# Segment mean: the general path rewritten with one-hot matmuls, the verdict for its branch read before the store, and part of the table work moved to GpSimd

## The chip, the cores and the metric

One core of one Trainium2 chip. The metric is the device time of one execution in microseconds, as the median of several. A profile gives a second clock, the span of the profiled execution, from its first record to its last; the device time is 1.77 us longer than that span in the kernel before. All times "at 190.66" below are microseconds from the start of the span. Repeats of one kernel scatter by up to 1.7%, and the chips differ by about 1%, so kernels are compared by ratios to runs of the kernel before on the same chip. An execution over 1.5% above the fastest of its kernel counts as slow and is left out of the ratio.

## The reference

```python
def reference(data, segment_ids):            # 10,000,000 float32, sorted ids in [0, 10000)
    num_segments = int(segment_ids.max()) + 1
    sums = np.zeros(num_segments, dtype=np.float32)
    counts = np.zeros(num_segments, dtype=np.float32)
    np.add.at(sums, segment_ids, data)
    np.add.at(counts, segment_ids, 1)
    return sums / np.maximum(counts, 1)
```

## The kernel before

The data are laid out as 128 partitions of 78,125 values, and each partition is cut into 98 "rows" of 800 values (the last has 525). The ids are sorted, and a segment holds about 1000 values, so a row usually contains one boundary between segments. The fast path finds that boundary with little reading of the ids: it reads a few probes, GpSimd gathers one window of 159 ids per row with a software DMA (98 gathers), ScalarE sums the window (the sum tells where the boundary lies), VectorE splits the row's data there, and ScalarE sums the whole row.

```python
def gather(g):
    for r in range(bounds[g], bounds[g + 1]):
        nc.gpsimd.indirect_dma_start(out=GT[:, r % RING, :], in_=ids2d[:], ...)   # 98 of these
def add_ids(r):                               # ScalarE: sum of the gathered window
    nc.scalar.activation(out=junk_a[:, 0:W], in_=gt32[:, r % RING, 0 : 2 * W : 2], func=ACT.Relu,
                         accum_out=GS[:, r : r + 1])
def second_look(a, b):                        # VectorE: where in the row the boundary lies
    def s1():
        nc.vector.tensor_sub(out=KK[:, a:b], in0=QQ[:, a:b], in1=GS[:, a:b])
    return [s1]
def total(r): ...                             # ScalarE: sum of the row's data
def split(r):                                 # VectorE: sum of the data before the boundary
    nc.vector.scalar_tensor_tensor(out=junk_v[:, 0:n], in0=iota[:, 0:n], scalar=KK[:, r : r + 1], in1=d,
                                   op0=ALU.is_lt, op1=ALU.mult, accum_out=A[:, r : r + 1])
```

Then the sums become segment means (`counts`, `sums`), and the means find their place in the output by compares and products (`select`, `table`, `place`; the last rows by `pick`). All of it is VectorE's. `check` and `verdict` find out whether the assumptions held; if not, the general path must do everything again. The answer of `verdict` is called the verdict here. `put(r, steps, k)` interleaves these steps behind row r, k steps to a row.

```python
    # ... cut ...
    put(75, sums(48, 72) + table(8, 13) + place(0, 40), 2)
    put(82, counts(72, R1))
    put(last_look + 1, keys(72, NX)[1:] + [check])          # check: GpSimd
    put(last_look + 3, select(13, NT1 // 4))
    put(89, sums(72, R1) + table(13, NT1 // 4) + place(40, C1) + place(C1, NO), 2)
    put(91, counts(R1, R3), 3)
    put(93, pick(sel1, R1, R2, C1), 3)
    put(94, pick(sel2, R2, R3, C2) + sums(R1, R2, False), 3)
    put(95, add_rows1(), 2)
    put(96, verdict())                                       # writes badi after the last split

def finish():
    # ... cut: the last sums and the last reduce ...
    for i, (src, dst) in enumerate(own_outputs(OUT, out2d[0:1, :])):
        (nc.scalar if i % 2 else nc.sync).dma_start(out=dst, in_=src)       # the output store
    with tc.If(nc.values_load(badi[0:1, 0:1], min_val=0, max_val=1) > 0):   # not taken here
        general_path(...)     # a running scan, then a binary search with indirect DMAs on GpSimd
```

With this input the branch is never taken, so how fast the general path would run plays no part in any time below.

Of the kernel before, what the change touches and what calls it, by code (L numbers as in the profile page):

```python
# [9 lines left out]
FP32 = mybir.dt.float32  # L10
# [7 lines left out]
P = 128  # L18
D = 78125
# [19 lines left out]
R1 = 84  # L39
R2 = 94  # L40
R3 = NR + 4
C1 = 50
C2 = 58


def general_path(tc, pool, ppool, data, segment_ids, ids2d, out2d, rdram, kdram, ident):


    nc = tc.nc
    N = data.shape[0]  # L50
    CH = 125
    data_p = data.rearrange("(p d) -> p d", p=P)
    ids_p = segment_ids.rearrange("(p d) -> p d", p=P)
    run_p = rdram.rearrange("(p d) u -> p (d u)", p=P)

    prev = pool.tile([P, 1], FP32, name="g_prev")
    rprev = pool.tile([P, 1], FP32, name="g_rprev")
    first = pool.tile([P, 1], FP32, name="g_first")
    f64 = pool.tile([P, 1], I64, name="g_f64")
    nc.sync.dma_start(out=f64, in_=ids_p[:, 0:1])  # L60
    nc.vector.tensor_copy(out=first, in_=f64.bitcast(I32)[:, 0:1])
    nc.vector.memset(prev, -1.0)
    nc.vector.memset(rprev, 0.0)
    with tc.For_i(0, D, CH) as c:
        i64 = pool.tile([P, CH], I64, name="g_i64")
        idf = pool.tile([P, CH + 1], FP32, name="g_idf")
        dat = pool.tile([P, CH], FP32, name="g_dat")
        msk = pool.tile([P, CH], FP32, name="g_msk")
        run = pool.tile([P, CH], FP32, name="g_run")
        nc.sync.dma_start(out=i64, in_=ids_p[:, bass.ds(c, CH)])  # L70
        nc.sync.dma_start(out=dat, in_=data_p[:, bass.ds(c, CH)])
        nc.vector.tensor_copy(out=idf[:, 0:1], in_=prev)
        nc.vector.tensor_copy(out=idf[:, 1 : CH + 1], in_=i64.bitcast(I32)[:, 0 : 2 * CH : 2])
        nc.vector.tensor_tensor(out=msk, in0=idf[:, 1 : CH + 1], in1=idf[:, 0:CH], op=ALU.is_equal)
        nc.vector.tensor_tensor_scan(
            out=run, data0=msk, data1=dat, initial=rprev[:, 0:1], op0=ALU.mult, op1=ALU.add
        )
        nc.vector.tensor_copy(out=prev, in_=idf[:, CH : CH + 1])
        nc.vector.tensor_copy(out=rprev, in_=run[:, CH - 1 : CH])
        nc.sync.dma_start(out=run_p[:, bass.ds(c, CH)], in_=run)  # L80


    pt = ppool.tile([1, 3 * P], FP32, name="g_pt")
    nc.tensor.transpose(out=pt[:, 0:P], in_=first, identity=ident)
    nc.tensor.transpose(out=pt[:, P : 2 * P], in_=prev, identity=ident)
    nc.tensor.transpose(out=pt[:, 2 * P : 3 * P], in_=rprev, identity=ident)
    row = pool.tile([1, 3 * P], FP32, name="g_row")
    nc.vector.tensor_copy(out=row, in_=pt)
    same = pool.tile([1, P], FP32, name="g_same")
    cont = pool.tile([1, P], FP32, name="g_cont")  # L90
    kd = pool.tile([1, P + 1], FP32, name="g_kd")
    nc.vector.memset(kd, 0.0)
    nc.vector.memset(cont, 0.0)
    nc.vector.tensor_tensor(out=same, in0=row[:, 0:P], in1=row[:, P : 2 * P], op=ALU.is_equal)
    nc.vector.tensor_tensor(
        out=cont[:, 1:P], in0=row[:, 1:P], in1=row[:, P : 2 * P - 1], op=ALU.is_equal
    )
    nc.vector.tensor_mul(out=cont, in0=cont, in1=same)
    nc.vector.tensor_tensor_scan(
        out=kd[:, 1 : P + 1], data0=cont, data1=row[:, 2 * P : 3 * P], initial=0.0,  # L100
        op0=ALU.mult, op1=ALU.add,
    )
    nc.sync.dma_start(out=kdram.rearrange("(u n) v -> u (n v)", u=1), in_=kd)

    Q = 125
    pedge = pool.tile([P, P], FP32, name="g_pedge")
    pe_i = pool.tile([P, P], I32, name="g_pei")
    nc.gpsimd.iota(pe_i, pattern=[[1, P]], base=1, channel_multiplier=0)
    nc.vector.tensor_scalar(out=pedge, in0=pe_i, scalar1=float(D), scalar2=None, op0=ALU.mult)
    seg = pool.tile([P, 2], FP32, name="g_seg")  # L110
    seg_i = pool.tile([P, 2], I32, name="g_segi")
    nc.gpsimd.iota(seg_i, pattern=[[1, 2]], base=0, channel_multiplier=80)
    nc.vector.tensor_copy(out=seg, in_=seg_i)
    means = pool.tile([P, 80], FP32, name="g_means")
    pos = pool.tile([P, 2], FP32, name="g_pos")
    step = pool.tile([P, 1], FP32, name="g_step")
    with tc.For_i(0, 80, 1) as q:
        nc.vector.memset(pos, 0.0)
        nc.vector.memset(step, float(1 << 23))
        with tc.For_i(0, 24, 1):  # L120
            cand = pool.tile([P, 2], FP32, name="g_cand")
            at = pool.tile([P, 2], FP32, name="g_at")
            at_i = pool.tile([P, 2], I32, name="g_ati")
            got = pool.tile([P, 2], I64, name="g_got")
            lt = pool.tile([P, 2], FP32, name="g_lt")
            ok = pool.tile([P, 2], FP32, name="g_ok")
            nc.vector.tensor_scalar(out=cand, in0=pos, scalar1=step[:, 0:1], scalar2=None, op0=ALU.add)
            nc.vector.tensor_scalar(
                out=at, in0=cand, scalar1=-1.0, scalar2=float(N - 1), op0=ALU.add, op1=ALU.min
            )  # L130
            nc.vector.tensor_copy(out=at_i, in_=at)
            for j in range(2):
                nc.gpsimd.indirect_dma_start(
                    out=got[:, j : j + 1], out_offset=None, in_=ids2d[:],
                    in_offset=bass.IndirectOffsetOnAxis(ap=at_i[:, j : j + 1], axis=0),
                )
            nc.vector.tensor_tensor(out=lt, in0=got.bitcast(I32)[:, 0:4:2], in1=seg, op=ALU.is_lt)
            nc.vector.tensor_scalar(out=ok, in0=cand, scalar1=float(N), scalar2=None, op0=ALU.is_le)
            nc.vector.tensor_mul(out=ok, in0=ok, in1=lt)
            nc.vector.scalar_tensor_tensor(  # L140
                out=pos, in0=ok, scalar=step[:, 0:1], in1=pos, op0=ALU.mult, op1=ALU.add
            )
            nc.vector.tensor_scalar(out=step, in0=step, scalar1=0.5, scalar2=None, op0=ALU.mult)
        last = pool.tile([P, 1], FP32, name="g_last")
        idx = pool.tile([P, 2], I32, name="g_idx")
        idxf = pool.tile([P, 2], FP32, name="g_idxf")
        val = pool.tile([P, 2], FP32, name="g_val")
        cnt = pool.tile([P, 1], FP32, name="g_cnt")
        some = pool.tile([P, 1], FP32, name="g_some")
        over = pool.tile([P, 1], FP32, name="g_over")  # L150
        jnk = pool.tile([P, P], FP32, name="g_jnk")
        nc.vector.tensor_scalar(
            out=idxf[:, 0:1], in0=pos[:, 1:2], scalar1=-1.0, scalar2=0.0, op0=ALU.add, op1=ALU.max
        )
        nc.vector.tensor_scalar(
            out=jnk, in0=pedge, scalar1=idxf[:, 0:1], scalar2=None, op0=ALU.is_le, op1=ALU.add,
            accum_out=idxf[:, 1:2],
        )
        nc.vector.tensor_copy(out=idx, in_=idxf)
        nc.gpsimd.indirect_dma_start(  # L160
            out=val[:, 0:1], out_offset=None, in_=rdram[:],
            in_offset=bass.IndirectOffsetOnAxis(ap=idx[:, 0:1], axis=0),
        )
        nc.gpsimd.indirect_dma_start(
            out=val[:, 1:2], out_offset=None, in_=kdram[:],
            in_offset=bass.IndirectOffsetOnAxis(ap=idx[:, 1:2], axis=0),
        )
        nc.vector.tensor_sub(out=cnt, in0=pos[:, 1:2], in1=pos[:, 0:1])
        nc.vector.tensor_scalar(out=some, in0=cnt, scalar1=0.0, scalar2=None, op0=ALU.is_gt)
        nc.vector.tensor_scalar(out=cnt, in0=cnt, scalar1=1.0, scalar2=None, op0=ALU.max)  # L170
        nc.vector.reciprocal(out=cnt, in_=cnt)
        nc.vector.tensor_mul(out=cnt, in0=cnt, in1=some)
        nc.vector.tensor_scalar(out=last, in0=idxf[:, 1:2], scalar1=float(D), scalar2=None, op0=ALU.mult)
        nc.vector.tensor_tensor(out=over, in0=pos[:, 0:1], in1=last, op=ALU.is_lt)
        nc.vector.tensor_mul(out=over, in0=over, in1=val[:, 1:2])
        nc.vector.tensor_add(out=over, in0=over, in1=val[:, 0:1])
        nc.vector.tensor_mul(out=means[:, bass.ds(q, 1)], in0=over, in1=cnt)
        nc.vector.tensor_scalar(out=seg, in0=seg, scalar1=1.0, scalar2=None, op0=ALU.add)
# [17 lines left out]
def kernel(  # L196
# [543 lines left out]
    def finish():  # L740
        n, m = NO - C2, R3 - R2
        for f in sums(R2, R3, False):
            f()
# [118 lines left out]
```

## Time and profile before

| | |
|---|---|
| median of 3 runs | 203.19 us (201.97 to 203.42) |
| profiled execution | 204.25 us, span 202.48 us |
| VectorE (DVE) busy | 140.4 us, 69% |
| ScalarE (ACT) busy | 138.2 us, 68% |
| GpSimd (POOL) busy | 106.9 us, 53% |

No engine is busy over 70%, because the limits follow one another. From the page of the kernel before: the busy times; then busy tenths in 40 slices of about 5 us; then the costliest groups (line, engine, operation, out<-in, shape, count, busy us, mean ns, idle us before them and what ended most of it).

```profile
PE 1.6 (1%) x6; PEld 1.4 (1%) x6; DVE 140.4 (69%) x537; ACT 138.2 (68%) x393; POOL 106.9 (53%) x135
...
DVE  6526197556684856695696849758597999899700
ACT  0042698986999967596797849689695988993000
POOL 5577747772765637174745535674645758810000
DMA  6999999999999999999999999999999999900000
...
L373 POOL DMA_INDIRECT GT<-in_segment_ids_dram,IDX x98 | 98.0, 1000 | 67.6 <-ACT junk_a L383 28.6
L403 DVE SCALAR_TENSOR_TENSOR junk_v<-iota,q_120,data_t 128x800 bf16<-128x800 f32 x98 | 102.0, 1041 | 31.8 <-DMA data_t<-in_data_dram 27.4
```

For about 35 slices the DMA row is full and the splits wait for their data. Then VectorE alone runs full, and the last two slices are empty on every engine. The table of stretches of the kernel before shows the same with the borders set at three events: VectorE's last wait for data (153.9), the landing of the last data (177.9), and the issue of the output store (191.43). Its columns are the stretch, its length, busy us of each engine, the clock, the DMA share and GB/s.

```profile
core 0: us, PE busy (x) PEld busy (x) DVE busy (x) ACT busy (x) POOL busy (x), PEclk, DMA share, GB/s
0.00:153.90 153.90, 0.99 (x4) 0.93 (x4) 104.28 (x420) 110.61 (x319) 90.62 (x103) 1.00 1.06 285
153.90:177.90 24.00, 0.00 (x0) 0.00 (x0) 23.20 (x77) 21.77 (x61) 16.21 (x32) 1.00 0.99 392
177.90:191.43 13.53, 0.59 (x2) 0.50 (x2) 12.91 (x42) 5.80 (x14) 0.09 (x1) 1.00 0.00 1
191.43:202.48 11.05, 0.00 (x0) 0.00 (x0) 0.00 (x0) 0.00 (x0) 0.00 (x0) 1.00 0.03 7
```

VectorE is busy 36.1 of the 37.5 us between 153.9 and 191.43. After that, 11 us in which no engine computes. The chain of work that ended last is of no help there: it follows compute and ends with VectorE's last reduce (191.05 + 0.35 us), so the tail has to be read from the instructions of the engines' sequencers (POOLq, SPq), the parts that issue the instructions, wait on semaphores (counters by which engines wait for each other) and branch. DRAIN is the name of such an instruction in the trace. These are the ones of the branch's line in the kernel before (count, duration in ns as minimum/median/maximum, first and last start), and then the DRAINs of the program's last line.

```profile
L750 POOLq COMPARE_BRANCH  x1: 45/45/45, 190.7 to 190.7; - x1
...
L750 POOLq INC_SWDGE_SEM  x1: 2146/2146/2146, 191.4 to 191.4; - x1
...
L750 SPq TENSOR_LOAD <-badi x1: 836/836/836, 193.0 to 193.0; - x1
...
L750 SPq COMPARE_BRANCH  x1: 50/50/50, 194.2 to 194.2; - x1
```

```profile
L857 POOLq DRAIN  x3: 40/107/8081, 193.6 to 202.2; - x3
L857 SPq DRAIN  x3: 7/7/13, 195.9 to 201.9; - x3
```

GpSimd branches at 190.66, spends 2.15 us in INC_SWDGE_SEM (which, by its name, increments a semaphore of the software DMA), and then spends 8.08 us in a DRAIN, from 193.56 to 201.64. SyncE, which has to issue the store (1.06 + 0.37 us), load the verdict and check it, is ready at 196.0 and waits 5.6 us for GpSimd. Barriers of 0.84 us follow. One label misleads here: the list of waits of the DMA queue's engine puts this wait down to PE, because PE's semaphore is the last of several to come; PE had long been done (its last matmul started at 189.51).

```profile
SPq L857 <- PEq L857: 6.4, 2, 5.8
```

### The profile page before, as it was taken

How to read it: one execution, taken by the hardware profiler on the slowest of the kernel's cores; microseconds unless marked ns; L12 is line 12 of the kernel's file. 1: busy time of each engine (PE TensorE's matmuls, PEld its weight loads, DVE VectorE, ACT ScalarE, POOL GpSimd, SP SyncE). 2: the span in 40 equal slices, each digit the busy share in tenths (PEclk: the TensorE clock that was granted, in tenths of full speed). 3: DMA queues.
4: the chain of work that ended last, by engine and by line, in shares of the span. 5: the costliest groups of instructions: out<-in, count | busy, mean ns of one | idle time of the engine just before them, and what ended most of it. 6: DMA issues, size and time to landing. Idle time of an engine off the chain costs nothing.

```text
span 202.5 us, 1634 instructions
## 1 busy us (share of the span) xinstructions
PE 1.6 (1%) x6; PEld 1.4 (1%) x6; DVE 140.4 (69%) x537; ACT 138.2 (68%) x393; POOL 106.9 (53%) x135
## 2 busy tenths in 40 slices
PE   0000000000001000000000000000000000000100
PEld 0000000000001000000000000000000000000000
DVE  6526197556684856695696849758597999899700
ACT  0042698986999967596797849689695988993000
POOL 5577747772765637174745535674645758810000
DMA  6999999999999999999999999999999999900000
GB/s 98 105 117 359 255 404 241 316 338 341 250 257 406 255 326 201 400 241 282 306 314 336 209 378 238 350 310 337 307 242 390 403 407 405 395 17 2 2 12 0
DMA packets 75143, 53.41 MB, mean 264 GB/s; under 512 B 65601, under 2 KB 65684, under 8 KB 75127
## 3 DMA queue, kind: packets, MB, share of 16 engines
q1 hardware_dynamic: 70249, 40.54, 71.8%
q0 software_dynamic: 4704, 12.74, 20.7%
q14 instruction: 16, 0.13, 0.2%
q10 hardware_dynamic: 174, 0.00, 0.1%
HBM read 56.46 MB, written 0.04 MB: 279 GB/s over the span
## 4 chain that ended last, share of the span: by engine, by line
DMA 36%; SPq 29%; issue 11%; DVE 8%; ACT 7%; POOL 2%; ACTq 0%; POOLq 0%; DVEq 0%
DMA data_t<-in_data_dram 24%; SPq L247 23%; DMA GT<-in_segment_ids_dram,IDX 12%; SPq L239 6%; ACT junk_a L398 4%; DVE junk_v L403 4%; ACT junk_a L383 3%; POOL GT L373 2%; DVE shf L688 0%; DVE tab L678 0%; DVE sel L673 0%; DVE add_150 L695 0%; DVE CS L602 0%; DVE FF L608 0%; DVE add_150 L726 0%
## 5 line engine op out<-in xcount | busy, mean ns | idle before, releaser
L373 POOL DMA_INDIRECT GT<-in_segment_ids_dram,IDX x98 | 98.0, 1000 | 67.6 <-ACT junk_a L383 28.6
L403 DVE SCALAR_TENSOR_TENSOR junk_v<-iota,q_120,data_t 128x800 bf16<-128x800 f32 x98 | 102.0, 1041 | 31.8 <-DMA data_t<-in_data_dram 27.4
L398 ACT ACTIVATE junk_a<-data_t 128x800 bf16<-128x800 f32 x98 | 85.0, 867 | 17.4 <-DMA data_t<-in_data_dram 10.7
L383 ACT ACTIVATE junk_a<-GT 128x159 bf16<-128x159 int32 x98 | 33.9, 346 | 18.6 <-DMA GT<-in_segment_ids_dram,IDX 10.7
L383 ACT ACTIVATION_READ_ACCUMULATOR junk_a<-GT 128x1 f32 x98 | 18.3, 187 | 0.0
L398 ACT ACTIVATION_READ_ACCUMULATOR junk_a<-data_t 128x1 f32 x98 | 18.2, 186 | 0.0
L390 DVE TENSOR_TENSOR q_120<-QQ,GS 128x5 f32<-128x5 f32 (+1 forms) x20 | 3.2, 162 | 13.8 <-issue 9.2
L403 DVE DVE_READ_ACCUMULATOR junk_v<-iota,q_120,data_t 128x1 f32 x98 | 8.3, 84 | 0.0
L383 ACT ACT_TABLE_LOAD x1 | 1.3, 1283 | 9.7 <-DVE q_120 L335 9.7
L329 DVE TENSOR_TENSOR eq<-pr 128x20 f32<-128x20 int32 (+1 forms) x20 | 3.5, 176 | 2.5 <-DMA pr<-in_segment_ids_dram 2.4
L342 DVE TENSOR_SCALAR NB<-q_120 128x5 f32<-128x5 f32 (+1 forms) x20 | 4.3, 215 | 0.0
L338 DVE TENSOR_SCALAR ST<-jc 128x5 f32<-128x5 f32 (+1 forms) x20 | 4.1, 204 | 0.0
L331 DVE CAST q_120<-pr 128x6 f32<-128x6 int32 (+2 forms) x20 | 3.9, 196 | 0.0
L334 DVE TENSOR_REDUCE jc<-eq 128x5 f32<-128x20 f32 (+1 forms) x20 | 3.4, 172 | 0.0
L352 DVE TENSOR_TENSOR pos<-ST,wb 128x5 f32<-128x5 f32 (+1 forms) x20 | 3.4, 168 | 0.0
L335 DVE TENSOR_TENSOR q_120<-q_120 128x5 f32<-128x5 f32 (+1 forms) x20 | 3.2, 160 | 0.0
L359 DVE SCALAR_TENSOR_TENSOR IDX<-NB,pos 128x5 int32<-128x5 f32 (+1 forms) x20 | 3.2, 160 | 0.0
L363 DVE SCALAR_TENSOR_TENSOR QQ<-NB,QQ 128x5 f32<-128x5 f32 (+1 forms) x20 | 3.2, 158 | 0.0
L353 DVE SCALAR_TENSOR_TENSOR QQ<-q_120,ST 128x5 f32<-128x5 f32 (+1 forms) x20 | 3.2, 158 | 0.0
L678 DVE TENSOR_REDUCE tab<-sel 128x32 f32<-128x384 f32 (+2 forms) x3 | 1.6, 534 | 0.1
L673 DVE TENSOR_TENSOR sel<-sel,RF 128x384 f32<-128x384 f32 (+2 forms) x3 | 1.6, 535 | 0.0
L664 DVE TENSOR_TENSOR sel<-KEY,jj 128x384 f32<-128x384 f32 (+2 forms) x3 | 1.6, 535 | 0.0
(113 smaller groups left out, 40.4 us busy)
## 6 DMA issues: line engine op xcount, KB each, us to landing
data_t<-in_data_dram SPq DMA_DIRECT2D x48, 800.0 KB
GT<-in_segment_ids_dram,IDX POOLq DMA_INDIRECT x98
pr<-in_segment_ids_dram SPq DMA_DIRECT2D x18, 25.0 KB
data_t<-in_data_dram SPq DMA_DIRECT2D x1, 400.0 KB
data_t<-in_data_dram SPq DMA_DIRECT2D x1, 262.5 KB
out_dram<-OUT SPq DMA_DIRECT2D x1, 36.6 KB
pr<-in_segment_ids_dram SPq DMA_DIRECT2D x1, 21.0 KB
pr<-in_segment_ids_dram SPq DMA_DIRECT2D x1, 18.0 KB
```

Of the source, the lines that this page charges most:

```text
L239: nc.sync.dma_start(out=pr_flat[:, a:b], in_=ids_p[:, a * S : (b - 1) * S + 1 : S])
L247: nc.sync.dma_start(out=d[:, 0 : c - a], in_=data_p[:, a:c])
L329: nc.vector.tensor_tensor(out=eq, in0=in0b, in1=in1b, op=ALU.is_equal)
L331: nc.vector.tensor_copy(out=V[:, a:e], in_=pr32[:, a:e, 0])
L334: nc.vector.tensor_reduce(out=jc, in_=eq, axis=AX.X, op=ALU.add)
L338: nc.vector.tensor_scalar(out=ST[:, a:b], in0=jc, scalar1=float(S), scalar2=float(1 + W), op0=ALU.mult, op1=ALU.add,)
L342: nc.vector.tensor_scalar(out=NB[:, a:b], in0=BT[:, a:b], scalar1=1.0, scalar2=None, op0=ALU.not_equal)
L352: nc.vector.tensor_add(out=pos, in0=ST[:, a:b], in1=wb[:, a:b])
L373: nc.gpsimd.indirect_dma_start(out=GT[:, r % RING, :], out_offset=None, in_=ids2d[:], in_offset=bass.IndirectOffsetOnAxis(ap=IDX[:, r : r ...
L383: nc.scalar.activation(out=junk_a[:, 0:W], in_=gt32[:, r % RING, 0 : 2 * W : 2], func=ACT.Relu, accum_out=GS[:, r : r + 1],)
L398: nc.scalar.activation(out=junk_a[:, 0:n], in_=d, func=ACT.Copy, accum_out=t)
L403: nc.vector.scalar_tensor_tensor(out=junk_v[:, 0:n], in0=iota[:, 0:n], scalar=KK[:, r : r + 1], in1=d, op0=ALU.is_lt, op1=ALU.mult, accum_ ...
```

## The change

The general path no longer uses GpSimd's DMA: it compares the upper and lower digits of each id with a ramp (one-hot vectors) and lets TensorE add up counts and sums in a 79x256 product. Without software DMA behind the branch, and with the verdict read into registers before the end, nothing should be left to do between the store and the end. Compares and products of the last table go to GpSimd, the middle table moves to rows 64 to 73, one block of rows less is handled separately at the end, and VectorE sums the gathered ids of rows 89 to 97 itself (ScalarE still sums them too). The checks go from GpSimd to VectorE, and a small store of the first outputs goes from ScalarE's queue, behind row 75, to SyncE's, later; the lines of that store and the body of the new check are cut below.

```diff
-def general_path(tc, pool, ppool, data, segment_ids, ids2d, out2d, rdram, kdram, ident):
+def general_path(tc, pool, ppool, data, segment_ids, out2d, ramp):
     # ... cut: out go the scan, the binary search and
-                nc.gpsimd.indirect_dma_start(out=got[:, j : j + 1], in_=ids2d[:], ...)
-        nc.gpsimd.indirect_dma_start(out=val[:, 0:1], in_=rdram[:], ...)
-        nc.gpsimd.indirect_dma_start(out=val[:, 1:2], in_=kdram[:], ...)
     # ... in come, per column of data:
+                nc.vector.tensor_scalar(out=oh, in0=ramp[:, 0:HI], scalar1=hi[:, at], op0=ALU.is_equal, ...)
+                nc.vector.tensor_scalar(out=ol[:, 0:LO], in0=ramp[:, 0:LO], scalar1=lo[:, at], op0=ALU.is_equal, ...)
+                nc.vector.tensor_scalar(out=ol[:, LO : 2 * LO], in0=ol[:, 0:LO], scalar1=dat[:, at], op0=ALU.mult, ...)
+                nc.tensor.matmul(out=prod, lhsT=oh, rhs=ol, start=u == 0, stop=u == U - 1)
@@
-R1 = 84
-R2 = 94
-R3 = NR + 4
+R1 = 94
+R2 = NR + 4
+ON_ACT = 89
@@ second_look
+                nc.vector.tensor_reduce(      # rows 89 to 97
+                    out=GS[:, c:e], in_=gt32[:, s : s + e - c, 0 : 2 * W : 2], axis=AX.X, op=ALU.add)
@@ select, table, place and pick take an engine; on GpSimd a compare is a subtract and an is_equal with 0
+            e.tensor_tensor(out=out, in0=in0, in1=in1, op=ALU.subtract)
+            e.tensor_scalar(out=out, in0=out, scalar1=0.0, scalar2=None, op0=ALU.is_equal)
@@ finish
-        with tc.If(nc.values_load(badi[0:1, 0:1], min_val=0, max_val=1) > 0):
+        with tc.If(verdict_reg[0] > 0):
@@ the schedule
-    put(75, sums(48, 72) + table(8, 13) + place(0, 40), 2)
-    put(82, counts(72, R1))
-    put(last_look + 1, keys(72, NX)[1:] + [check])
-    put(last_look + 3, select(13, NT1 // 4))
-    put(89, sums(72, R1) + table(13, NT1 // 4) + place(40, C1) + place(C1, NO), 2)
-    put(91, counts(R1, R3), 3)
-    put(93, pick(sel1, R1, R2, C1), 3)
-    put(94, pick(sel2, R2, R3, C2) + sums(R1, R2, False), 3)
-    put(95, add_rows1(), 2)
-    put(96, verdict())
+    put(64, counts(48, 66), 2)
+    put(67, sums(48, 66) + table(8, 12, v) + place(0, 36, v), 2)
+    put(60, check(), 2)                                          # check: VectorE
+    put(last_look + 1, keys(MID, NX)[1:] + check_late())
+    put(last_look + 2, select(12, NT1 // 4, g))
+    put(last_look + 2, pick()[:1])
+    put(91, counts(66, R2), 3)
+    put(93, pick()[1:])
+    put(93, sums(66, R1), 4)
+    t, p = table(12, NT1 // 4, g), place(36, NO, g)
+    put(93, t[:1])
+    put(95, t[1:] + p[:1], 2)
+    put(96, p[1:])
+    put(94, verdict())
+    after[96].append(lambda: verdict_reg.append(nc.values_load(badi[0:1, 0:1], min_val=0, max_val=1)))
```

## The prediction

> **What bounds the kernel now.** Three stretches. (a) To about 154 us it runs at the pace of the loads: the splits (VectorE, 800 columns, 0.97 us start to start in the timeline) wait for data_t, 27 us in the list of waits. (b) From 153.9 to 191.4 us VectorE never waits for anything but its own previous result: the data have landed by 178 us and ScalarE ends at 183.9, but VectorE still has the tables, picks and last rows to do. (c) From the output store (191.43) to 202.5 us nothing computes. The branch's and the end's own lines show why: GpSimd starts INC_SWDGE_SEM at 191.38 (2.15 us) and then a DRAIN of 8.08 us, to 201.64; SyncE is ready at 196.0. Barriers (0.8 us) follow. So 5.6 us of the tail are GpSimd's alone.
>
> **What changes.**
> 1. No software DMA in the general path: INC_SWDGE_SEM disappears from GpSimd's program. I take the long DRAIN to belong to it (at the start of the kernel the same pair takes 0.03 and 0.17 us).
> 2. The verdict is read before the last split, so SyncE no longer does register load, checks and branch set-up (about 1.2 us) after the store. Store issue 1.49, branch and 18 semaphore waits about 1.9, barriers 0.8-1.0: tail about 4.4 us instead of 11.05. **-6.7 us.** If the DRAIN stayed 8 us it would begin some 6 us earlier with the earlier verdict, and the loss would be only about 1.5 us.
> 3. VectorE after 153.9: removed are the last select (0.57), its product (0.69), both place products (0.9), picks and adds of two blocks (about 3.5, one block of 0.75 stays), separate counts and sums of rows 72-83 and 84-93 (about 2), and the middle table, moved into the load-bound stretch (about 2.5). Added: two sums of the gathered ids on VectorE (795 and 636 elements, 0.9 and 0.75 us), check_late and two products (0.7).
> 4. But ScalarE still sums all 98 windows, so VectorE's sums of rows 89 to 97 wait for ScalarE's write. ScalarE's sum of row 93 ended at 169.8; VectorE will want it at about 167.6. VectorE should idle about 2 us there and 0.5 us before the second sum.
> 5. GpSimd gets 528-, 168- and 559-element operations. From the trace a tensor_tensor of 122 takes 0.40 and one of 1 takes 0.19 us, so about 1.75 ns an element (the Trainium skill, "GPSIMD Engine Reference", section 3.1, says about 2.6 cycles, a little slower); estimates 1.1 to 1.2 us for each large product. The place product may hold VectorE 0.3 us.
> 6. ScalarE no longer waits about 1.7 us for its small store (153.9): its end moves up by 0.5-1 us.
>
> By start-to-start times of like instructions, VectorE's last reduce ends near 188.6 instead of 191.4: **-2.8 us**.
>
> **Prediction: 194.0 us, 8 in 10 from 191.5 to 197.5.** Faster by over 2%: 0.95; within 2%: 0.04; slower: 0.01.
>
> **What would show it:** no INC_SWDGE_SEM at the end and GpSimd's last DRAIN under 1 us; end of the span 4 to 5 us after the store's issue; VectorE idle before its sums of GT; last reduce at 187.5-189.5; splits up to row 75 at unchanged times.
>
> **What would make it wrong:** the DRAIN is a cost of any software DMA (then about 195.5); GpSimd's selects run far slower than estimated and hold up the last table; the register load on VectorE stalls the last split by more than 0.2 us; ScalarE, waiting for the verdict, becomes last; the loads land later.

## The result, and the profile after

The changed kernel takes 196.28 us (195.87 to 197.04, 4 runs) against 203.31 us (201.97 to 203.77, 4 runs) of the kernel before of the same rounds. The ratio is 0.966, with a 95% interval of 0.961 to 0.971. A ratio here is the mean time of one kernel's fast runs over that of the other's of the same rounds, so not quite the ratio of these medians. In a later comparison, with six runs of it, the ratio was 0.964 (0.960 to 0.969). The prediction was 194.0 us, in a range of 191.5 to 197.5.

The lines of the page after the change that answer to those of before:

```profile
PE 1.6 (1%) x6; PEld 1.4 (1%) x6; DVE 139.9 (72%) x541; ACT 138.1 (71%) x393; POOL 108.0 (55%) x121
...
DVE  6535197874775867495967686967999679899960
ACT  0043398985999998595968686866978779999310
POOL 5487737775467573746456373737383674850410
DMA  6999999999999999999999999999999999993000
...
L290 POOL DMA_INDIRECT GT<-in_segment_ids_dram,IDX x98 | 98.3, 1003 | 66.2 <-ACT junk_a L300 31.2
L333 DVE SCALAR_TENSOR_TENSOR junk_v<-iota,q_118,data_t 128x800 bf16<-128x800 f32 x98 | 102.1, 1042 | 26.8 <-DMA data_t<-in_data_dram 23.7
```

The table of stretches of the kernel after, with the borders at the like events (the same split starts at 153.15 instead of 153.86, the store is issued at 188.97):

```profile
0.00:153.20 153.20, 0.99 (x4) 0.93 (x4) 108.12 (x444) 111.06 (x321) 90.29 (x103) 1.00 1.06 286
153.20:177.30 24.10, 0.00 (x0) 0.00 (x0) 20.98 (x64) 21.63 (x61) 14.69 (x16) 1.00 1.00 395
177.30:188.97 11.67, 0.59 (x2) 0.50 (x2) 10.75 (x34) 5.44 (x12) 3.07 (x3) 1.00 0.01 4
188.97:194.88 5.91, 0.00 (x0) 0.00 (x0) 0.00 (x0) 0.00 (x0) 0.00 (x0) 1.00 0.04 8
```

The tail has shrunk from 11.05 to 5.91 us and the two stretches before it from 37.5 to 35.8 us. The branch's line of the kernel after, and the DRAINs of its last line:

```profile
L711 POOLq COMPARE_BRANCH  x1: 45/45/45, 185.2 to 185.2; - x1
...
L711 SPq COMPARE_BRANCH  x1: 50/50/50, 190.5 to 190.5; - x1
```

```profile
L824 POOLq DRAIN  x3: 40/113/8409, 185.6 to 194.6; - x3
L824 SPq DRAIN  x3: 7/7/7, 192.0 to 194.3; - x3
```

INC_SWDGE_SEM is gone, but the long DRAIN is not: it takes 8.41 us, now from 185.62 to 194.03. (GpSimd's last product ran until 185.93, so 8.10 us of it follow GpSimd's last work, where it was 8.08 before.) SyncE is ready at 192.09, 1.94 us before GpSimd. So the end is still GpSimd's; only it starts 5.5 us earlier, and from the branch to the end it is 2.1 us shorter. In the list of waits of the DMA queue's engine, after the change:

```profile
SPq L824 <- PEq L824: 2.7, 2, 2.1
```

VectorE's last reduce ends at 188.94. What VectorE waited for from 153.3 to 188.97 in the kernel after (us in total, times, longest):

```profile
DVE junk_v L333 <- DMA data_t<-in_data_dram: 3.6, 4, 1.3
DVE GS L311 <- ACT junk_a L300: 0.5, 1, 0.5
DVE OUT L675 <- POOL shf L668: 0.4, 1, 0.4
DVE junk_v L333 <- DVE j_163 L440: 0.2, 1, 0.2
```

And in the kernel before, from 154 to 191.43 (the 1.3 us end at 153.86, at the border, so they are not inside it):

```profile
DVE junk_v L403 <- DMA data_t<-in_data_dram: 1.3, 1, 1.3
DVE q_120 L390 <- ACT junk_a L383: 0.6, 1, 0.6
```

VectorE's busy time in these two stretches fell by 4.4 us (23.20 + 12.91 against 20.98 + 10.75), but only 1.8 us of that shortened them. Work taken away before 168 us was partly turned into waits for loads: of the 3.6 us, 1.3 us lie at the border as before, and 2.3 us are new, from 155.6, 159.4 and 164.8 on. That this comes with the rearranged work is seen across the runs: all eight profiles that have it and all 98 gathers show such waits after row 76 (1.2 to 2.3 us, counting waits over 0.12 us), and the three with the old work (before, e1, e2) show none.

### The profile page after: what moved, and what is told of

Its sections match the earlier page's. It is cut to its first block, busy times and chain, and to the rows that moved or that the text cites. A ratio compares the mean times of both kernels' runs of the same rounds, so it can differ in the third digit from the quotient of the medians.

```text
span 194.9 us, 1624 instructions
## 1 busy us (share of the span) xinstructions
PE 1.6 (1%) x6; PEld 1.4 (1%) x6; DVE 139.9 (72%) x541; ACT 138.1 (71%) x393; POOL 108.0 (55%) x121
## 4 chain that ended last, share of the span: by engine, by line
DMA 31%; SPq 30%; issue 14%; DVE 10%; ACT 10%; POOL 3%; POOLq 0%; DVEq 0%; ACTq 0%
SPq L162 24%; DMA data_t<-in_data_dram 23%; DMA GT<-in_segment_ids_dram,IDX 7%; SPq L154 6%; ACT junk_a L328 5%; DVE junk_v L333 5%; ACT junk_a L300 4%; POOL GT L290 2%; POOL shf L668 1%; DVE CS L577 1%; DVE tab L658 0%; DVE GS L311 0%; DVE ct L559 0%; DVE FF L583 0%; DVE q_118 L574 0%
## 5 line engine op out<-in xcount | busy, mean ns | idle before, releaser
L695 POOL TENSOR_TENSOR pk<-pk,RB 128x168 f32<-128x168 f32 x1 | 0.5, 507 | 7.2 <-DVE q_118 L574 7.2
L259 DVE TENSOR_SCALAR NB<-q_118 128x5 f32<-128x5 f32 (+1 forms) x20 | 3.5, 176 | 0.0
L255 DVE TENSOR_SCALAR ST<-jc 128x5 f32<-128x5 f32 (+1 forms) x20 | 3.5, 174 | 0.0
L311 DVE TENSOR_REDUCE GS<-GT 128x5 f32<-128x795 int32 (+1 forms) x2 | 1.8, 899 | 0.6 <-ACT junk_a L300 0.5
L668 POOL TENSOR_TENSOR shf<-tab,dm 128x559 f32<-128x559 f32 x1 | 1.3, 1332 | 1.4 <-DVE badi L528 1.4
```

Of the source, the lines that this page charges most:

```text
L255: nc.vector.tensor_scalar(out=ST[:, a:b], in0=jc, scalar1=float(S), scalar2=float(1 + W), op0=ALU.mult, op1=ALU.add,)
L259: nc.vector.tensor_scalar(out=NB[:, a:b], in0=BT[:, a:b], scalar1=1.0, scalar2=None, op0=ALU.not_equal)
```

## The experiments

Ten runs, of nine kernels, were made on three chips, on which the kernel before took 205.74, 205.09 and 205.35 us. Ratios compare each with the kernel before on its own chip. Two events decide when each kernel ends: GpSimd's end of its long DRAIN, and SyncE's readiness. All from the profiles, in us; "work" is from the start of the split of row 76 to the end of VectorE's last reduce.

| profile | work | last reduce ends | GpSimd's DRAIN ends | SyncE ready | end of span |
|---|---|---|---|---|---|
| before | 37.54 | 191.40 | 201.64 | 196.00 | 202.48 |
| after | 35.79 | 188.94 | 194.03 | 192.09 | 194.88 |
| e1_path_only | 37.61 | 193.83 | 201.72 | 197.92 | 202.57 |
| e2_verdict_early | 38.51 | 193.35 | 193.55 | 197.17 | 198.00 |
| e3_drain_early | 35.10 | 190.69 | 187.75 | 193.84 | 194.67 |
| e4_no_dve_sums | 33.77 | 187.93 | 193.01 | 191.08 | 193.87 |
| e5_compute_only | 35.44 | 189.95 | 200.22 | 194.54 | 201.06 |
| e6_half_gathers | 35.80 | 179.41 | 180.49 | 182.55 | 183.39 |
| e7_best | 34.16 | 189.18 | 191.30 | 192.32 | 193.16 |
| e8_no_act_sums | 34.69 | 188.06 | 193.16 | 191.22 | 194.01 |
| after_again | 35.19 | 190.33 | 195.43 | 193.49 | 196.28 |
| e7_again | 34.04 | 190.12 | 192.25 | 193.27 | 194.10 |

In all twelve rows the end of the span is the later of the two events plus 0.83 to 0.86 us (after: 194.03 + 0.85; e2: 197.17 + 0.83). That is the whole account of the end of this program, and each experiment moves one or more of its terms. The main theory: the long DRAIN is owed for the 98 gathers of the fast path, whatever lies behind the branch, and it ended the kernel both before and after.

### e1_path_only: the kernel before with the new general path alone

```diff
-            general_path(tc, fpool, ppool, data, segment_ids, ids2d, out2d, rdram, kdram, ident[:, 0:P])
+            general_path(tc, fpool, ppool, data, segment_ids, out2d, iota)
```

> The kernel before with the new general path alone. Theory D: the long DRAIN of GpSimd is owed for the gathers, lasts about 8.1 us after GpSimd's last work whatever stands in the branch, and starts when GpSimd has passed the branch. Then INC_SWDGE_SEM (2.15 us) goes, the DRAIN stays at 8.0 to 8.4 us and starts near 191.2 in the span, and the time falls by 2.0 to 2.5 us (ratio to the kernel before 0.988 to 0.990). Rival I (of the prediction): the DRAIN belongs to INC_SWDGE_SEM; then the last DRAIN is under 1 us and the time falls by about 5.5 us (ratio 0.973).

Measured: 202.75 us, ratio 0.984 (0.978 to 0.990), unclear at the limit of 2%; the interval holds the 0.988 of the main theory and not the 0.973 of the prediction's reading. Its profile fell in a run that counts as slow (204.34 us, over 1.5% above the fastest), so its span is not compared, only what its end consists of. INC_SWDGE_SEM is absent behind the branch, and the DRAINs of the last line are:

```profile
L772 POOLq DRAIN  x3: 40/107/8157, 193.6 to 202.3; - x3
L772 SPq DRAIN  x3: 7/7/7, 197.9 to 202.0; - x3
```

The general path owns the 2.15 us of INC_SWDGE_SEM and not the DRAIN. From GpSimd's branch (193.10) to the end are 9.47 us, against 11.82 us in the kernel before: 2.35 us less, and 8.16 us of DRAIN are still there. The prediction's assumption that the two belong together falls.

### e2_verdict_early: the kernel before, with the verdict earlier and nothing else

```diff
-        with tc.If(nc.values_load(badi[0:1, 0:1], min_val=0, max_val=1) > 0):
+        with tc.If(verdict_reg[0] > 0):
@@
-    put(96, verdict())
+    put(91, verdict())
+    after[94].append(lambda: verdict_reg.append(nc.values_load(badi[0:1, 0:1], min_val=0, max_val=1)))
```

> The kernel before, old general path, with its verdict moved from after row 96 to after rows 91 and 92 and the register load to row 94; no work is taken from VectorE. Theory D: GpSimd passes the branch near 182 instead of 190.7, INC_SWDGE_SEM and the 8.1 us DRAIN are over near 192.5, and SyncE, ready 3.1 us after the store's issue near 191.4, becomes last: span about 195.3, time 6 to 7.5 us less than before (ratio 0.963 to 0.971), about as much as the whole change. Rival V: the change's gain comes from the work taken off VectorE and from the path; then only SyncE's register load is saved, at most 1.2 us (ratio 0.994 or more).

Measured: 199.23 us, ratio 0.968 (0.962 to 0.975), so as much as the whole change gives, with the old general path and no work taken off VectorE. GpSimd's branch moved from 190.66 to 182.55, and INC_SWDGE_SEM and the DRAIN, still 2.15 and 8.08 us long, ran beside VectorE's last rows:

```profile
L859 POOLq DRAIN  x3: 40/107/8081, 185.5 to 197.7; - x3
L859 SPq DRAIN  x3: 7/7/13, 197.1 to 197.4; - x3
```

GpSimd is done at 193.55, SyncE at 197.17. The end has changed hands. The rival, that a gain of this size needs VectorE's saved work, falls. The span of this profile, 198.00, was expected at 195.3: VectorE's last reduce came 2 us later than in the kernel before (1.0 us of it at the split of row 76 already), which was not looked into.

### e3_drain_early: the changed kernel, with a DRAIN on GpSimd in the middle

```diff
     put(last_look + 2, pick()[:1])
+    put(last_look + 2, [lambda: nc.gpsimd.drain()])
```

> The changed kernel with one more drain on GpSimd, after the compares of the last pick, where GpSimd idles from 173.6 to 180.8. Theory D: this drain takes about 8.1 us and ends near 181.7, the last one is then under 0.5 us, SyncE (192.1 in the changed kernel) is last, and the time is 1.7 to 2.3 us under the changed kernel's (ratio to the kernel before about 0.955). Rival F: a DRAIN at the end has a fixed cost; then the last one is still 8 us and the time is that of the changed kernel (0.966) or more.

Measured: 196.14 us, ratio 0.954 (0.951 to 0.957); the change itself has 0.966 and 0.964 in its two comparisons. The added DRAIN, and those of the last line:

```profile
L754 POOLq DRAIN  x1: 8780/8780/8780, 174.1 to 174.1; - x1
```

```profile
L825 POOLq DRAIN  x3: 34/112/346, 187.4 to 194.4; - x3
L825 SPq DRAIN  x3: 7/7/7, 193.8 to 194.1; - x3
```

The cost can be paid once, earlier: 8.78 us at 174.1, while GpSimd had nothing urgent to do (for 0.68 us of it the last compare still ran, so 8.10 us follow GpSimd's work, as at the end of the changed kernel), and then 0.35 us at the end (during which its last product still ended). So it is not a fixed price of ending the program. With it out of the way, the end comes 3.98 us after VectorE's last reduce (190.69 to 194.67), not the 5.94 us of the changed kernel. The prediction had 4.4 us for this tail, so its sum for SyncE's share was 0.4 us too high.

### e4_no_dve_sums: the changed kernel, with the window sums left to ScalarE alone

```diff
-ON_ACT = 89
+ON_ACT = NR
@@
-        put(a - 2 if a < ON_ACT else a - 3 if b < NR else a - 4, second_look(a, b))
+        put(a - 2 if b < NR else a - 3, second_look(a, b))
```

> The changed kernel without VectorE's sums of gathered ids for rows 89 to 97 (ScalarE's sums, which it makes anyway, are used, as in the kernel before). Theory S: those sums, their products and their waits for ScalarE cost VectorE about 2.7 us (0.90 + 0.73 + 0.43 + 0.65) on the way to the verdict and to the store; both move up by 2.0 to 2.7 us and so does the end (ratio to before 0.953 to 0.957). Rival: VectorE only waits elsewhere for ScalarE or the data; then less than 1 us is gained (0.962 or more).

Measured: 195.85 us, ratio 0.957 (0.950 to 0.964). In the changed kernel ScalarE sums the windows of rows 89 to 97 too, and VectorE's sums, which write the same tile, wait for that. Without them VectorE's work of the last rows takes 33.77 us, against 35.79 and 35.19 us in the two profiles of the changed kernel: 1.4 to 2.0 us less, where 2.0 to 2.7 were expected. (A product of 30 elements took 1.40 us here, against 0.37 and 0.20 us there, which takes back about 1 us; see the last section.) The sums bought nothing here: they cost VectorE 1.6 us (0.90 and 0.73, start to start) plus their waits, and give ScalarE nothing back.

### e5_compute_only: the changed kernel's work with the old general path and the old, late verdict

```diff
-        with tc.If(verdict_reg[0] > 0):
-            general_path(tc, fpool, ppool, data, segment_ids, out2d, iota)
+        with tc.If(nc.values_load(badi[0:1, 0:1], min_val=0, max_val=1) > 0):
+            general_path(tc, fpool, ppool, data, segment_ids, ids2d, out2d, rdram, kdram, ident[:, 0:P])
@@
-    put(94, verdict())
-    after[96].append(lambda: verdict_reg.append(nc.values_load(badi[0:1, 0:1], min_val=0, max_val=1)))
+    put(96, verdict())
```

> The changed kernel with the old general path and the verdict read after the store, as before: only the rearranged work. Theory D: VectorE's last reduce ends about 2.5 us earlier than in the kernel before, the verdict is the last but five of its results, so GpSimd passes the branch near 188.3, INC_SWDGE_SEM and the 8.1 us DRAIN follow, and the end moves by the same 2.0 to 3.0 us (ratio to before 0.985 to 0.990), SyncE idling some 5 us before it. If more than 0.980 is reached, the work taken off VectorE is worth more than its own time.

Measured: 202.99 us, ratio 0.987 (0.982 to 0.993). The interval leaves out 1: the work moved off VectorE is worth 1.3% alone. GpSimd's branch is at 189.22, since the verdict comes sooner, and the whole tail of before follows (INC_SWDGE_SEM 2.15 us, DRAIN 8.08 us to 200.22).

The parts do not add up: 1.6% (path), 3.2% (verdict), 1.3% (work) make 6.1%, and the change gives 3.4 to 3.6%. They all shorten or advance the same chain on GpSimd, from the branch to the end of the DRAIN, and once that chain is about as short as SyncE's, more of it gains nothing. What the new path adds to the whole change was not measured: no run has the changed kernel with the old path and the early verdict. Since GpSimd is last there, an estimate is the 2.15 us of INC_SWDGE_SEM (before, e2, e5).

### e6_half_gathers: the changed kernel with every second gather left out

Its output is wrong, which doesn't matter for the time. The tile of windows is zeroed and the odd rows never filled.

```diff
     for r in range(bounds[g], bounds[g + 1]):
+            if r % 2:
+                continue
             nc.gpsimd.indirect_dma_start(
```

> The changed kernel with the gathers of even rows only (49 of 98; the result is wrong on purpose, odd rows sum stale windows). Theory D1: the last DRAIN is owed per gather; it lasts 4.0 to 4.6 us. Rival D2: it has a fixed length once any gather was issued; 8.0 to 8.4 us.

Measured once (its state is unknown): 185.4 us.

```profile
L827 POOLq DRAIN  x3: 40/113/4372, 176.1 to 183.1; - x3
```

Half the gathers, half the DRAIN: 4.37 us, of which 4.10 follow the end of GpSimd's last product, against 8.10 us with 98. That is 84 and 83 ns per gather (4.10 / 49 and 8.10 / 98). A cost that does not depend on the number of gathers is excluded. The gathers are all alike, so whether the cost goes by the gather, by its packets or by its bytes isn't told apart. The time of the whole, 185.4 us, says nothing about the tail: with less to fetch, the split of row 76 started at 143.61 instead of 153.15.

### e7_best: what the experiments suggest, together

The changed kernel with the window sums left to ScalarE (as in e4), the last place product back on VectorE, and the verdict four rows earlier, so that GpSimd reaches its DRAIN sooner.

```diff
-ON_ACT = 89
+ON_ACT = NR
     # ... cut: the same line of second_look as in e4
-    t, p = table(12, NT1 // 4, g), place(36, NO, g)
+    t, p = table(12, NT1 // 4, g), place(36, NO, v)
-    put(94, verdict())
-    after[96].append(lambda: verdict_reg.append(nc.values_load(badi[0:1, 0:1], min_val=0, max_val=1)))
+    put(90, verdict())
+    after[94].append(lambda: verdict_reg.append(nc.values_load(badi[0:1, 0:1], min_val=0, max_val=1)))
```

> The changed kernel without VectorE's sums of ids (as in the run without them), with the verdict made after rows 90 and 91 and loaded after row 94, and the last place product back on VectorE, so that GpSimd's last work is the product of the last table near 181. Theory D: its DRAIN is over near 190, no longer last; SyncE is last, 3.1 us plus 0.8 us of barriers after the store's issue near 187.2; span about 191, ratio to before 0.943 to 0.950, faster than the changed kernel (0.966) by 1.6 to 2.3%. If the DRAIN starts late all the same, or ScalarE's or VectorE's waits return, 0.957 (the run without the sums) is the bound.

Measured: 195.16 us, ratio 0.950 (0.944 to 0.956).

```profile
L824 POOLq DRAIN  x3: 40/113/8355, 182.9 to 192.9; - x3
L824 SPq DRAIN  x3: 7/7/7, 192.3 to 192.6; - x3
```

GpSimd is done at 191.30, SyncE at 192.32, and the tail after the last reduce is 3.98 us as in e3. The ratio is at the upper edge of what was expected; the interval overlaps with those of e3 and e4, so that the three edits together beat each of these isn't shown.

### e8_no_act_sums: the changed kernel, with ScalarE's sums of rows 89 to 97 left out

```diff
-        while r >= -1 and gs < min(r + 1 + X_SUM, NR):
+        while r >= -1 and gs < min(r + 1 + X_SUM, ON_ACT):
             add_ids(gs)
```

> The changed kernel with ScalarE's sums of rows 89 to 97 left out, so that VectorE's are the only ones. Theory S: VectorE's waits before the two sums (0.65 us) go, the 1.63 us of the sums stay; 0.3 to 0.8 us gained on the changed kernel (ratio to before 0.962 to 0.964). ScalarE ends about 4 us earlier up to its last total, which waits for the verdict all the same. Rival: the doubled work on ScalarE sets the end; then 2 us or more are gained.

Measured: 196.62 us, ratio 0.956 (0.950 to 0.963). VectorE's waits before its two sums are gone, as expected, and its work of the last rows is 34.69 us, 0.5 to 1.1 us less than in the two profiles of the changed kernel. The ratio came out lower than expected, and the expected values lie at the edge of its interval. Since the changed kernel itself was not run on this chip, the size of this effect is not settled.

### after_again and e7_again: the change and e7_best on one chip

Both kernels unchanged, five rounds each.

> The changed kernel once more, on the same chip as the next run. Its ratio to the kernel before should be 0.956 to 0.969 again, with GpSimd last: a DRAIN of about 8.1 us counted from the end of its last product.

> The same kernel as in the run that combined the three edits, for a direct comparison with the changed kernel. Theory D: SyncE last; 1.0 to 2.0% under the changed kernel of the same chip (ratio to before 0.945 to 0.955). If the two ratios' intervals overlap by more than half, the gain isn't shown.

Measured: 197.93 us, ratio 0.964 (0.960 to 0.969), for the change; 194.56 us, ratio 0.949 (0.943 to 0.954), for e7_best. The intervals do not overlap: e7_best beats both kernels, and is 1.6% below the change (0.949 / 0.964). In these two profiles the changed kernel ends 5.95 us after its last reduce, with GpSimd last, and e7_best 3.98 us after, with SyncE last.

## Why the prediction was right, and where it was not

**The bound named in the prediction held.** The tail of 11 us after the store was the place to gain, most of it was GpSimd's, and both the prediction and the runs show it: the 7.6 us of span gained between the two profiles (202.48 to 194.88) all lie in the shift of one chain. GpSimd's branch came 5.5 us earlier (190.66 to 185.18), and from there to the end it was 2.1 us shorter (11.82 to 9.70).

**The step that failed** is the one the prediction put as "I take the long DRAIN to belong to it", that is, to INC_SWDGE_SEM. From it followed "GpSimd's last DRAIN under 1 us" and "tail about 4.4 us". The DRAIN stayed 8.4 us (e1: 8.16 us with the general path's DMA gone), costs 83 to 84 ns for each gather of the fast path (e6), and kept the tail at 5.94 us, counted from the end of the last reduce. The clue that was used for the wrong step was right in itself: at the start of the program the same pair takes 0.03 and 0.17 us. But there no gather has been issued yet, which the prediction did not consider.

**Why it was near all the same.** The prediction named this case: "If the DRAIN stayed 8 us it would begin some 6 us earlier with the earlier verdict, and the loss would be only about 1.5 us", and "then about 195.5". The DRAIN began 7.9 us earlier (193.56 to 185.62) and the tail was 5.94 - 4.4 = 1.5 us longer than predicted. The cost did not go away. It was hidden behind VectorE's last work, except for 1.94 us. So the number was near by luck as far as the DRAIN goes: in this schedule its right and its wrong reading differ by only some 2 us in the end. The prediction chose the wrong one, and only named the other.

**The sum, term by term.** The prediction has 188.6 (last reduce) + 4.4 (tail) = 193.0, and says 194.0, which leaves an unstated 1.0 from span to median time. The runs have 188.94 + 5.94 = 194.88 and a median 1.40 above that span. Of the 2.28 us that it was low, 1.54 are the tail (1.96 for the DRAIN, less the 0.42 by which SyncE's share was put too high: 5.94 - 3.98 and 4.4 - 3.98, with e3's tail), 0.34 VectorE, and 0.40 the step from span to time. The last has two parts, neither of them in the prediction: the profiled execution of the kernel before was about 1 us above its median (204.25 against 203.2 to 203.3 us), that of the kernel after only 0.76 us above its own; and the difference between time and span, 1.77 us before, is 2.15 us after. It is 2.15 to 2.16 us in e3 and e8 too, 1.76 to 1.78 us in e1, e2, e4, e5 and e7, and 2.01 us in e6. What makes it so was not looked for.

**VectorE: the right end, with different parts.** The last reduce was predicted at 188.6 and came at 188.94, 2.5 us earlier than before. Of these, 0.7 us were there before the split of row 76 (153.86 to 153.15), which the prediction expected unchanged; other profiles with all gathers have that split anywhere from 153.4 to 156.2, so this is scatter, and luck. The work from there on is 1.75 us shorter, and 2.35 us in the second profile of the change, instead of 2.8 us. Removed work before 168 us turned into waits for loads, 2.3 us (1.2 us in the second profile of the change): the change lengthened the load-bound stretch, which the prediction had ended at 154 us. The waits for ScalarE before the window sums were predicted as 2 and 0.5 us and are 0.47 and 0.10 us (1.01 and 0.33 in the second profile). In the first profile VectorE, held by the loads, came to the first sum at 168.7 instead of 167.6, and ScalarE had row 93 ready at 169.1 instead of 169.7. That these waits and sums were on VectorE's path is shown by e4 (1.4 to 2.0 us). One forecast missed without consequence: ScalarE's end was to move up by 0.5 to 1 us and came 2.1 us later (183.88 to 185.95), since its last total now stands behind the load of the verdict (3.09 us idle); the chain that ended last does not go through it there.

**GpSimd's work held nothing up but the last place.** The last table's product of 528 elements took 1.23 us and the place product of 559 elements 1.33 us, against estimates of 1.1 to 1.2; VectorE waited 0.45 us for the latter, predicted 0.3. In the chain of work that ended last after the change, it stands right before VectorE's last operations:

```profile
184.60 1.34 POOL shf L668
185.94 0.02 issue
185.96 0.45 DVE OUT L675
```

The Trainium skill ("GPSIMD Engine Reference", section 3.1) has about 2.6 cycles at 1.2 GHz for an element with two inputs, which makes an estimate of 1.1 us for 528 elements before any fixed cost. The whole products agree with that well; the prediction's estimate of 1.75 ns per element, from two small operations of the trace, was a little low.

## What to carry to other kernels

Where an engine has issued software DMAs, look for its DRAIN at the end of the program, count it per DMA, and ask where it starts: it is paid from the engine's own last instruction on, so the last thing that this engine waits for (here a verdict that it only had to read) should come as early as possible, or the DRAIN should be paid where the engine is idle. Two edits of one to three lines gained as much as the whole change (e2: 3.2%) and about 1% on top of it (e3), where the rearranged work alone gave 1.3% (e5). The parts did not add up, because all of them act on one chain: write down the candidates for the last event, and stop when another one leads. And work taken away from a stretch that waits for loads can return as waiting, as 1.2 to 2.3 us did here.

## What the Trainium skill lacked or had wrong

- No page has the cost of GpSimd's DRAIN after software DMAs. "VectorE: DVE Perf Modes", section "The DRAIN you can't avoid", describes the boilerplate DRAINs of the program's start and end as about 12 ns and constant, on all five engines. That agrees here with SyncE (7 to 13 ns), VectorE (10 to 17 ns) and PE (8 ns), not with one of ScalarE's at the end (65 to 361 ns); GpSimd's takes 8.1 us after 98 gathers and 4.10 us after 49, 83 to 84 ns for each, and it can be paid earlier (8.78 us at 174.1, then 0.35 us at the end).
- No page has INC_SWDGE_SEM, which GpSimd executes when it passes a branch over code with software DMA that is not taken: 2.15 us in each of the three profiles that have the old general path (before, e2, e5), absent there in the others (at the start of the program it takes 0.03 us in all of them).
- "GPSIMD Engine Reference", section 4.1, calls one-input operations on GpSimd roughly line-rate. The is_equal with a constant on 528 elements took 1.55 us, longer than the product of two inputs of the same size (1.23 us). In the kernel before, a multiplication by a constant on 122 elements took 0.57 us and a product of two inputs of that size 0.40 us.
- "GPSIMD Engine Reference", section 1, says that GpSimd shares its SBUF interfaces with VectorE and that VectorE's instructions with two SBUF inputs contend. No gap of the skill as a whole is claimed here; the traces agree only in part. VectorE's product of 30 elements, which takes 0.20 us in one profile of the changed kernel, took 1.50 us in e7_best and 1.40 us in e4, beside GpSimd's operations on 528 elements, and the scan of 28 took 0.57 us beside a GpSimd product and 0.28 us without. In five profiles (after, e4, e7_best, e7_again, e8) that product ended 0.06 us after GpSimd's subtraction of 528 elements did. But the splits of 800 columns, which also have two SBUF inputs, kept their 1.03 to 1.05 us beside GpSimd's operations with two inputs. That GpSimd is the cause was read from the coincidence in time and not tested by an experiment.
